# Routing decisions of an expert layer: one comparison each, the arm that is usual placed straight behind it, and two pieces of shared work placed ahead

## Chip, cores and metric

The kernel runs on one core of a Trainium2 chip. The metric is the device time of one execution in microseconds. Five engines run their own instruction streams: TensorE (PE in the profile, its weight loads PEld), VectorE (DVE), ScalarE (ACT), GpSimd (POOL) and SyncE (SP, which issues nearly all DMAs). [...]

## What is computed

A two-layer backbone over 256 latent and 256 context tokens of width 1024. Each layer mixes tokens (windowed attention, pooling, retention, one output projection) and then applies a gated channel mixer: dense in layer 0, and in layer 1, for the 256 latent tokens, two of eight experts per token. The change lies in that last mixer:

```python
def swiglu(t, wg, wu, wd):
    return (jax.nn.silu(t @ wg) * (t @ wu)) @ wd

def moe_ffn(t, router, wg, wu, wd):
    logits = (tf @ router).astype(jnp.float32)
    top_v, top_i = lax.top_k(logits, TOP_K)          # TOP_K = 2, N_EXPERTS = 8
    top_w = jax.nn.softmax(top_v, axis=-1)
    gates = ...                                      # top_w at the two chosen experts, 0 elsewhere
    for e in range(N_EXPERTS):
        y = y + gates[:, e:e + 1] * swiglu(tf, wg[e], wu[e], wd[e])
```

All is float32. FFN_DIM is 2816, so one expert has 34.6 MB of weights.

## The kernel before

Up to the experts the program is straight. The router's products, the choice of two experts per token and the numbers of tokens per expert are computed on the chip at about 834 to 838 us of the profiled execution. What follows depends on these numbers, so the kernel reads them into registers and branches.

Each expert's weights come in 11 parts of 3 MB (`FC` = 11; a part holds 256 hidden features: gate and up in `RGU`, down in `RD`, which are the tiles `rgu` and `raw`, or in further buffers `p` for the first expert). An expert with its tokens is called a place. Place 0 is expert 0, whose weights are loaded before its number of tokens is known. Places 1 to 7 are the others by falling number of tokens, in an order that depends on how many have more than 128.

- **First decision (lines 2483 to 2495).** `number[0]`, the tokens of expert 0, is loaded into a register of every engine (`tokens_of`, line 2480), and nested conditions (lines 2484, 2485, 2492) choose one of four arms: more than 128 tokens (two blocks), at most 128, at most 64, at most 32. Each arm is a whole copy of `first_place`. It begins with `first_block(m)`: the tokens are gathered as rows by a product with a one-hot matrix `OG[0]` (`og`), copied to `HP` (`hx`), turned by transposes and multiplied by the modulation `G12`, `B12`. With m = 32, four column parts of TensorE are used side by side, 256 columns of features each. Then 11 parts are multiplied. Beside them, as generators that are advanced between the products, run `modulated` (what the other experts read), `ranks` (places and registers' contents, on DVE), `beside_first` (gathering for places 1 and 2) and `residuals`.
- **Between the decisions (lines 2499 to 2507).** SP reads seven experts' numbers and six part numbers into registers, then issues the loads of parts `FC` and `FC + 1`, the first of the next place. Every engine reads four token numbers.
- **Second decision (lines 2508 to 2528).** Nested conditions choose one of seven arms: `group` (a place of two blocks and one or two small places beside it, by turns) and `places` (one after the other). `group` begins by splitting its first part into high and low halves (`split_g`: ACT writes `ghi`, DVE writes `glo`; `split_d` does the same for the down weights) and with the product `gate_up` of the first block.

The arms stand in the program in the order of the text, an `Else` behind its `If`. The arms that ran in the profiled execution are the last `Else` of the first decision (m = 32) and the `Else` at line 2525 (`group(1, [2, 3], 32, True)`, then `places` for 4 to 7). The join behind an arm that stands last is the next instruction; behind any other arm stands an unconditional branch to the join. In the trace taken branches of both kinds appear as COMPARE_BRANCH on the line of their condition. Almost all instructions are recorded by a helper at line 280 (281 in the changed kernel).

Of the kernel before, what the change touches and what calls it, by code (L numbers as in the profile page):

```python
# [30 lines left out]
D = 1024  # L31
T = 256
# [20 lines left out]
# used all along, and by the mixers only  # L53
_CA, _NA = _table(("ident", 128), ("before", 128), ("slots", 128),
                  ("eless", 64), ("eidx", 8), ("order", 32), ("first", 8))
# [4 lines left out]
def _constants():  # L60
# [44 lines left out]
    put("first", np.where(e == 0, 1024.0, 0.0)[None, :])  # L105
    return ca, cb, cc
# [12 lines left out]
# ---------------------------------------------------------------- layouts of the inputs  # L119
# vec: per layer  b_mod 48 | ln1_g 8 | ln1_b 8 | ln2_g 8 | ln2_b 8 | pool_scale 2 | sink 8 | lg_f 4 | lg_b 4  # L120
# [7 lines left out]
def prep(x, c, ctx, c_ctx, w_mod, b_mod, w_in, attn_sink, pool_w, pool_scale, ret_log_decay_fwd,  # L128
# [13 lines left out]
    # shift and scale of the first mixer by feature tile: [tile, p, k, shift|scale, 128]  # L142
# [127 lines left out]
class Engine:  # L270
    """an engine whose instructions are noted"""
# [65 lines left out]
def build(tc, a, dbg=None):  # L337
# [19 lines left out]
    # ---- what stays on chip all along  # L357
# [3 lines left out]
    XT = con.tile([128, KT, NT], F32, name="XT")   # alpha times the residual stream, feature-major  # L361
    HH = con.tile([128, KT, NT], F32R, name="HH")  # hi and lo parts of what goes into the next product
# [34 lines left out]
    # ---- the stream of weights of the dense part: the order in which they are used  # L397
# [3 lines left out]
    def weave(ws, ms, every):  # L401
        """after the i-th of the weights every[i] of the others"""
# [7 lines left out]
    WEAVE0 = [8, 5, 3, 0]                   # beside the input projection of layer 0  # L410
    WEAVEF = [0, 2, 2, 2] + [1] * 18        # beside gate and up
# [16 lines left out]
    def split_piece():  # L428
        """take the next granule apart, a part after the other"""
# [19 lines left out]
    def split_next(ahead=1):  # L449
        """take the next granule apart, if it is a weight and less than `ahead` wait for their use"""  # L450
# [4 lines left out]
    def pump(ahead=1):  # L455
        """go on with the granule to take apart when it has come and the engines for it have nothing else to do"""
# [24 lines left out]
    def next_weights(out, hold=False):  # L481
# [3 lines left out]
        pos["held"] = hold              # nothing more is taken apart while two granules are in use  # L485
# [43 lines left out]
    fixed = {}                  # of some kinds of small tiles, those that are there by turns  # L529
# [13 lines left out]
    def scales(l, which, g=None, b=None):  # L543
        """G, B with  modulated = xn * G + B  (xn before the norm's own g, b)"""
# [21 lines left out]
    def stats(k, h, st):  # L566
        """add the feature tile k of XT into the sums of the norm"""
# [60 lines left out]
    def apply_norm(k, h, nm):  # L628
        """two feature tiles from k on"""
# [9 lines left out]
    def modulate(k, h, gb, slot=None):  # L639
        """xn * G + B for two feature tiles, where their lo part comes later"""  # L640
# [12 lines left out]
    def feed(h, nm, gb):  # L653
        """a half of the tokens, normed and modulated, to where the products read it"""
# [9 lines left out]
    # ------------------------------------------------------------------ the mixer  # L664
# [13 lines left out]
    def open_late(t, eng):  # L678
        """what is not needed by the first part of the input projection"""
# [18 lines left out]
    def decay(l, DJ):  # L698
        """the decays of the retention, within a stream (DL) and from the context to the latents (DC)"""
# [30 lines left out]
    def chunked(t, w, i, s):  # L730
        """128 columns of the input projection for the tokens s, in four parts; the bank goes to t["out"]"""
# [35 lines left out]
    def values_flip(t, b, m0, n):  # L767
        """the values from feature-major to token-major"""
# [206 lines left out]
    def finish(t):  # L975
        """hi and lo parts of the mixed heads, once the input projection has read what they replace"""
# [18 lines left out]
    def sums(h, sts, done):  # L995
        """the sums of the norm of a half of the tokens, each feature tile after its residual is in"""
# [965 lines left out]
    def first_place(m, again, side, before=True):  # L1962
# [5 lines left out]
        if before:  # L1968
            first_block(m)
# [579 lines left out]
```

## Time and profile before

| what | value |
|---|---|
| time, median of 3 runs | 1625.1 us (1619.96 to 1629.07) |
| span of the profiled execution | 1624.5 us |
| PE busy | 1482.4 us (91%) |
| DVE busy | 741.4 us (46%) |
| ACT busy | 614.2 us (38%) |
| DMA | 398.67 MB, mean 245 GB/s |
| chain that ended last | PE 78%, DVE 9%, ACT 5%, DMA 4%, issue 3% |

The span lies 0.6 us below the median, so a sum made against the profiled execution is carried over by adding 0.6 us. In the page's 40 slices of 40.6 us PE is busy nine tenths or more in most; it falls off where the layers' attention is and around the two decisions. "Issue" in the chain is time in which an engine waited for nothing that the profile shows. The experts' stage runs from about 838 us to the end.

### The profile page before, as it was taken

To read this page: it belongs to the slowest core of one execution; us is meant where nothing else is said; L and a number is where in the kernel's file an instruction comes from. 1 tells how busy PE (TensorE), PEld (TensorE's weight loads), DVE (VectorE), ACT (ScalarE), POOL (GpSimd) and SP (SyncE) were. 2 spreads that over 40 slices of the span, in tenths; PEclk is the share of its full clock that TensorE was granted. 3 is DMA by queue.
4 is the path that set the end of the run, shared out by engine and by line. 5 is a ranking of instruction groups with operands and counts; after the bars stand their busy time and mean duration, and the time that the engine had idled before them with its cause. 6 is when DMAs were issued, how large, how long until landed. Compare 5 with 4: busy or idle time off the path is not lost.

```text
span 1624.5 us, 25303 instructions
## 1 busy us (share of the span) xinstructions
PE 1482.4 (91%) x10390; PEld 1088.8 (67%) x10390; DVE 741.4 (46%) x1426; ACT 614.2 (38%) x1121; POOL 93.8 (6%) x105
## 2 busy tenths in 40 slices
PE   6989999999999999887968499999998879999986
PEld 4646677777777788675746377777774458878643
DVE  4664456223223343666435344243323158888412
ACT  3464444522222343355531133232321047767301
POOL 2310002000000420100000100000000000000120
PEclk9999999999999999999988799999999999999999
DMA  9444223554444332231468689999998998988894
GB/s 380 169 157 182 103 104 108 210 202 170 175 173 164 121 128 92 100 133 43 173 270 349 255 316 374 373 361 378 358 378 318 372 370 310 362 329 326 336 398 197
DMA packets 45727, 398.67 MB, mean 245 GB/s; under 512 B 5600, under 2 KB 5856, under 8 KB 8960
## 3 DMA queue, kind: packets, MB, share of 16 engines
q1 hardware_dynamic: 44640, 391.97, 62.5%
q0 software_dynamic: 640, 4.26, 0.7%
q8 instruction: 94, 1.54, 0.4%
q14 instruction: 65, 0.53, 0.1%
q10 hardware_dynamic: 288, 0.36, 0.1%
HBM read 395.53 MB, written 1.05 MB: 244 GB/s over the span
## 4 chain that ended last, share of the span: by engine, by line
PE 78%; DVE 9%; ACT 5%; DMA 4%; issue 3%; SPq 0%; ACTq 0%; POOL 0%; DVEq 0%; POOLq 0%
PE bk L280 40%; PE b L280 38%; DMA rgu<-in_moe_dram 2%; DVE nm L280 2%; DVE XT L280 2%; ACT pexp L280 2%; DVE wl L280 1%; DMA raw<-in_wmod_dram 1%; DVE pexp L280 1%; DMA ar<-in_wm_dram 1%; ACT wh L280 1%; ACT pair L280 1%; DVE HL L280 0%; DVE hx L280 0%; DVE b L280 0%
## 5 line engine op out<-in xcount | busy, mean ns | idle before, releaser
L280 PE MATMUL b<-HH,wh 128*128 128x512 f32 (+1 forms) x752 | 268.3, 357 | 7.9 <-ACT wh L280 6.5
L280 PE MATMUL b<-HL,wh 128*128 128x512 f32 (+1 forms) x752 | 258.7, 344 | 1.1 <-DVE HL L280 1.1
L280 PE MATMUL b<-HH,wl 128*128 128x512 f32 (+1 forms) x752 | 259.0, 344 | 0.7 <-DVE wl L280 0.6
L280 DVE TENSOR_TENSOR wl<-raw,wh 128x512 fp32r<-128x512 f32 x228 | 150.5, 701 | 125.1 <-ACT wh L280 124.9
L280 PE MATMUL bk<-ghi,HL 128*128 128x512 f32 x528 | 182.3, 408 | 20.5 <-ACT ghi L280 20.5
L280 PEld LDWEIGHTS b<-HH,wh 128*128 128x128 f32 x752 | 143.5, 191 | 64.9 <-issue 26.4
L280 ACT ACTIVATE wh<-raw 128x512 fp32r<-128x512 f32 x228 | 132.9, 623 | 117.4 <-PE b L280 63.3
L280 DVE TENSOR_TENSOR glo<-rgu,ghi 128x1024 fp32r<-128x1024 f32 x132 | 154.7, 1218 | 28.6 <-ACT ghi L280 28.4
L280 PEld LDWEIGHTS b<-HH,wl 128*128 128x128 f32 x752 | 143.6, 191 | 19.4 <-DVE wl L280 2.2
L280 PEld LDWEIGHTS b<-HL,wh 128*128 128x128 f32 x752 | 143.8, 191 | 17.1 <-DVE HL L280 1.9
L280 ACT ACTIVATE hx<-bk 128x256 f32<-128x256 f32 (+2 forms) x88 | 27.7, 315 | 306.9 <-PE bk L280 301.9
L280 ACT ACTIVATE ghi<-rgu 128x1024 fp32r<-128x1024 f32 x132 | 131.2, 1051 | 30.4 <-issue 18.7
L280 DVE TENSOR_TENSOR hx<-hx,bk 128x256 f32<-128x256 f32 (+2 forms) x88 | 29.5, 335 | 236.8 <-ACT hx L280 236.8
L280 PEld LDWEIGHTS bk<-ghi,HL 128*128 128x128 f32 x528 | 101.6, 192 | 49.9 <-issue 22.9
L280 PE MATMUL bk<-dhi,SP 128*128 128x512 f32 x352 | 119.5, 400 | 0.0
L280 PE MATMUL b<-h,wh 128*128 128x512 f32 (+1 forms) x384 | 111.9, 375 | 0.0
L280 PE MATMUL bk<-glo,HL 128*128 128x512 f32 x264 | 105.8, 401 | 2.0 <-DVE glo L280 2.0
L280 DVE TENSOR_TENSOR H<-H,b 128x512 f32<-128x512 f32 x22 | 15.1, 687 | 167.5 <-PE b L280 157.4
L280 DVE TENSOR_TENSOR dlo<-raw,dhi 128x1024 fp32r<-128x1024 f32 (+1 forms) x55 | 78.7, 1433 | 15.8 <-ACT dhi L280 15.8
L280 PE MATMUL bk<-rgu,hx 128*32 128x128 f32 (+1 forms) x1376 | 80.6, 315 | 5.4 <-DVE hx L280 2.9
L280 PEld LDWEIGHTS b<-h,wh 128*128 128x128 f32 x384 | 69.8, 188 | 16.4 <-issue 2.5
L280 PEld LDWEIGHTS bk<-rgu,hx 128*32 128x32 f32 (+1 forms) x1376 | 55.0, 122 | 37.6 <-issue 14.5
(329 smaller groups left out, 2178.6 us busy)
## 6 DMA issues: line engine op xcount, KB each, us to landing
rgu<-in_moe_dram SPq DMA_DIRECT2D x81, 2048.0 KB, 9.7
raw<-in_moe_dram SPq DMA_DIRECT2D x80, 1024.0 KB, 7.6
raw<-in_wmod_dram SPq DMA_DIRECT2D x40, 1024.0 KB, 4.8
raw<-in_fgu_dram SPq DMA_DIRECT2D x22, 1024.0 KB, 5.5
p<-in_moe_dram SPq DMA_DIRECT2D x16, 1024.0 KB, 14.7
raw<-in_wout_dram SPq DMA_DIRECT2D x12, 1024.0 KB, 4.8
raw<-in_fd_dram SPq DMA_DIRECT2D x11, 1024.0 KB, 4.8
raw<-in_wib_dram SPq DMA_DIRECT2D x9, 1024.0 KB, 4.9
```

The costliest lines, as they stand in the source:

```text
L280: r = f(*args, **kw)
```

## The change

The first decision now hangs on one number, computed on DVE (`kind`: how many of 32, 64 and 128 are exceeded), the second likewise (`over`, `C1`, an arm's number from 0 to 6). Each decision compares it once with the usual arm's number; that arm stands directly behind the comparison, and the other arms behind it, in a chain of further comparisons. `first_block` no longer depends on the arm: it gathers 128 tokens whatever their number, and stands ahead of the first condition. The first product of place 1 (`next_first`: the splits of part `FC`, `gate_up` of its first block, `split_d`) stands ahead of the second condition; `group` and `places` skip it. Between the decisions SP reads one expert's number, issues the loads of part `FC`, reads two part numbers, issues those of part `FC + 1`, and reads the other ten registers after that. Comments were taken out as well.

```diff
-    V.tensor_copy(C0, b[:, 2 * E:2 * E + 1])
+    kind = rt.tile([128, 4], F32, name="kind")
+    V.tensor_scalar(kind[:, :3], cst("steps"), b[:, 2 * E:2 * E + 1], None, op0=OP.is_lt)
+    V.reduce_sum(kind[:, 3:], kind[:, :3], axis=AX.X)
+    V.tensor_copy(C0, kind[:, 3:])
...
-    def first_block(m):
...
+    def first_block():
+        og = OG[0].bitcast(F32)
+        for h in range(2):
             for i in range(2):
-                for j in range(n):
...
+                P.matmul(halved(BK[h]), lhsT=og[:, i], rhs=XN[:, i, 2 * h:2 * h + 2], start=i == 0, stop=i == 1)
+        for h in range(2):
+            if h:
+                S.activation(HP[h], BK[h], AF.Copy)
             else:
+                V.tensor_copy(HP[h], BK[h])
+            for c in range(4):
+                P.transpose(BK[2 + h][:, 128 * c:128 * c + 128], HP[h][:, 128 * c:128 * c + 128], IDENT)
+        x, b = (t.rearrange("p (k q) -> p k q", q=128) for t in (HP[0], BK[2]))
+        for t, r, op in ((b, G12, OP.mult), (x, B12, OP.add)):
+            V.tensor_tensor(x, t, r[:, 0:4, 0:1].to_broadcast([128, 4, 128]), op)
+        for k in range(4):
+            c = slice(128 * k, 128 * k + 128)
+            S.activation(HP[1][:, c], BK[3][:, c], AF.Identity, scale=G12[:, 4 + k, 0:1], bias=B12[:, 4 + k, 0:1])
...
-        if s == 1:
+        if s > 1:
+            run(split_g(u0, 0, 2))
...
+        else:
             one_hot_few(pos_of(few[0]), m)
             from_stash(m)
...
-        V.tensor_copy(CNTI[:, :2], BP[:, 4:6])
+        V.tensor_scalar(over[:, 0:2], BP[:, 4, 3:5], 64.0, None, op0=OP.is_gt)
+        V.tensor_scalar(over[:, 2:3], BP[:, 4, 3:4], 32.0, None, op0=OP.is_gt)
+        V.scalar_tensor_tensor(over[:, 3:4], many[:, 5:6], 1.0, many[:, 3:4], op0=OP.add, op1=OP.mult)
+        V.scalar_tensor_tensor(over[:, 2:3], over[:, 1:2], 2.0, over[:, 2:3], op0=OP.mult, op1=OP.max)
+        V.scalar_tensor_tensor(over[:, 3:4], over[:, 3:4], 3.0, over[:, 2:3], op0=OP.add, op1=OP.subtract)
+        V.scalar_tensor_tensor(over[:, 3:4], over[:, 3:4], over[:, 0:1], over[:, 2:3], op0=OP.mult, op1=OP.add)
+        V.scalar_tensor_tensor(C1, over[:, 3:4], 1.0, many[:, 1:2], op0=OP.add, op1=OP.mult)
+        V.tensor_copy(CNTI[:, 1:2], BP[:, 5:6])
...
+    def arms(arm, usual, bodies, shared):
+        shared()
+        with tc.If(arm == usual, preferred_fallthrough_block=True) as c:
+            bodies[usual]()
+        with c.Else():
+            one_of(arm, [x for x in bodies.items() if x[0] != usual])
...
+    arms(arm_of(C0[0:1, 0:1], 4), 0, {0: lambda: first(32), 1: lambda: first(64), 2: lambda: first(128), 3: first_twice},
+         first_block)
...
-    for s in range(1, E):
-        eid[s] = nc.values_load(CNTI[0:1, 1, s:s + 1], engines=[ET.SP], min_val=0, max_val=E - 1)
...
-    number.update({s: tokens_of(s) for s in (1, 3, 4, 5)})
...
+    expert_of(1)
+    load_gu(FC)
+    load_d(FC)
+    parts_of(1)
+    load_gu(FC + 1)
+    load_d(FC + 1)
+    arm = arm_of(C1[0:1, 0:1], 7)
+    def next_first():
+        for s in range(2, E):
+            expert_of(s)
+        for s in (3, 5):
+            parts_of(s)
         for i in range(2):
+            run(split_g(FC, i, 2))
+            gate_up(FC, 1, range(4 * i, 4 * i + 4), BK[6])
+        run(split_d(FC))
...
+    arms(arm, 1, {0: lambda: places([(s, False) for s in range(1, E)], [], True),
+                  1: lambda: places(few_ends, group(1, [2, 3], 32, True)),
...
+                  5: two_groups, 6: three_groups}, next_first)
```

On PE the first decision stands like this before. `SELR` is the router's choice, `XT,og` the gathering product, `CA,hx` a transpose of the gathered rows, `rgu,hx` the first gate and up product. The rows with the last width of 32 are the arm that ran; it stands last of the four.

```order
L280 MATMUL b<-SELR,SP 128x8 x2
L2480 TENSOR_LOAD C_6481
L2484 COMPARE_AND_BRANCH
L2485 COMPARE_AND_BRANCH
L280 MATMUL bk_6512<-XT,og 128x512 x2
...
L2485 UNCONDITIONAL_BRANCH
L2492 COMPARE_AND_BRANCH
L280 MATMUL bk_6512<-XT,og 64x512 x4
...
L2492 UNCONDITIONAL_BRANCH
L280 MATMUL bk_6512<-XT,og 32x256 x8
L280 MATMUL bk_6514<-CA,hx 128x128 x2
L280 MATMUL bk_6516<-rgu_5029,hx 32x128 x32
```

The gathering and its transposes now come between the register load and the one comparison, and the arm of width 32 comes straight behind it. On PE, now:

```order
L281 MATMUL b<-SELR,SP 128x8 x2
L2483 TENSOR_LOAD C_6481
L281 MATMUL bk_6515<-XT,og 128x512 x2
L281 MATMUL bk_6516<-XT,og 128x512 x2
L281 MATMUL bk_6517<-CA,hx 128x128 x4
L281 MATMUL bk_6518<-CA,hx 128x128 x4
L2498 COMPARE_AND_BRANCH
L281 MATMUL bk_6519<-rgu_5029,hx 32x128 x32
```

Eight products of 32 by 256, which ran four side by side, became four of 128 by 512, and two transposes became eight.

On PE the end of the first place and the second decision stand like this before. `os,HL` brings the first place's outputs to the tokens, `ghi,HL` is the first product of the next place.

```order
L280 MATMUL bk_6519<-os_6501,HL 128x256 x4
L2492 UNCONDITIONAL_BRANCH
L2480 TENSOR_LOAD CNTI x4
L2508 COMPARE_AND_BRANCH
L2509 COMPARE_AND_BRANCH
L2510 COMPARE_AND_BRANCH
L280 MATMUL bk_6518<-ghi_8991,HL 128x512
...
L2523 UNCONDITIONAL_BRANCH
L280 MATMUL bk_6518<-ghi_8991,HL 128x512
```

The register loads follow the first place's arm directly, and three comparisons at lines 2509, 2520 and 2523 lead to an arm far down. On PE, now:

```order
L281 MATMUL bk_6522<-os_6504,HL 128x256 x4
L2498 UNCONDITIONAL_BRANCH
L2490 COMPARE_AND_BRANCH
L281 MATMUL bk_6519<-rgu_5029,hx 64x256 x16
...
L2490 UNCONDITIONAL_BRANCH
L2483 TENSOR_LOAD C_6540
L281 MATMUL bk_6521<-ghi_8972,HL 128x512
...
L2498 COMPARE_AND_BRANCH
L281 MATMUL bk_6519<-IDR,og 128x128 x2
```

Behind the usual arm of the first decision there is now an unconditional branch over the three other arms, 990 matmuls on PE, 440 instructions on DVE and 142 on ACT; the 24 matmuls of the first product stand ahead of the second comparison, whose usual arm follows it.

## Rows read from the trace of the kernel before

**Rows 1.** Chain of work that ended last, both decisions: start us, us, what.
```profile
840.85 8.91 issue
...
914.88 6.04 issue
...
927.51 4.90 issue
...
932.57 1.06 ACT ghi L280
...
933.72 1.24 DVE glo L280
...
935.00 13.31 PE bk L280 x103
```

**Rows 2.** Branches by line: duration ns min/median/max, first and last start us.
```profile
L2484 PEldq COMPARE_BRANCH  x1: 6414/6414/6414, 838.0 to 838.0; - x1
L2484 DVEq COMPARE_BRANCH  x1: 72/72/72, 838.1 to 838.1; - x1
...
L2484 ACTq COMPARE_BRANCH  x1: 55/55/55, 839.8 to 839.8; - x1
...
L2492 ACTq COMPARE_BRANCH  x1: 45/45/45, 840.3 to 840.3; - x1
L2492 DVEq COMPARE_BRANCH  x1: 56/56/56, 843.9 to 843.9; - x1
L2492 PEldq COMPARE_BRANCH  x1: 5072/5072/5072, 844.5 to 844.5; - x1
...
L2508 PEldq COMPARE_BRANCH  x1: 70/70/70, 916.2 to 916.2; - x1
...
L2509 PEldq COMPARE_BRANCH  x1: 6232/6232/6232, 916.3 to 916.3; - x1
```

**Rows 3.** Timeline from the first decision: start us, us, engine, operation, idle before.
```profile
837.39 0.47 DVE L280 TENSOR_SCALAR og<-CA,NAT 128x128 fp32r<-128x128 f32 x2
...
849.76 1.94 PE L280 MATMUL bk<-XT,og 128*32 128x256 f32 x16 [12.64 <-issue]
...
852.34 0.69 PE L280 MATMUL bk<-CA,hx 128*128 128x128 f32 x2 [0.64 <-DVE hx L280]
...
853.78 3.64 PE L280 MATMUL bk<-rgu,hx 128*32 128x128 f32 x64 [0.76 <-PE bk L280]
...
859.00 1.08 PE L280 MATMUL bk<-rgu,hx 128*32 128x128 f32 x32
...
865.44 0.69 DVE L280 TENSOR_TENSOR XT<-XT,bk 128x512 f32<-128x512 f32 x1
```

**Rows 4.** Stretches: busy us of PE, PEld, DVE, ACT, POOL; granted clock, DMA share, GB/s.
```profile
838.00:849.50 11.50, 0.00 (x0) 0.00 (x0) 0.00 (x0) 2.80 (x5) 0.00 (x0) 0.51 0.58 231
853.50:857.50 4.00, 3.72 (x65) 3.37 (x66) 0.18 (x1) 1.16 (x5) 0.00 (x0) 0.50 0.02 4
933.60:940.50 6.90, 6.27 (x14) 4.62 (x15) 6.78 (x5) 4.67 (x5) 0.00 (x0) 0.50 0.19 44
1000.00:1200.00 200.00, 199.94 (x1998) 150.70 (x2000) 78.22 (x118) 64.26 (x97) 0.00 (x0) 1.00 0.93 369
```

**Rows 5.** Timeline of DVE and PE behind the ranking of the experts.
```profile
877.70 0.17 DVE L280 SCALAR_TENSOR_TENSOR steps<-steps 128x7 f32<-128x7 f32 x1
...
878.96 0.67 PE L280 MATMUL bk<-IDR,og 128*128 128x128 f32 x2 [3.50 <-DVE og L280]
```

**Rows 6.** Register loads of lines 2480 and 2500, columns as in rows 2.
```profile
L2480 ACTq TENSOR_LOAD <-CNTI x4: 275/284/289, 913.4 to 914.4; - x4
...
L2480 PEldq TENSOR_LOAD <-CNTI x4: 300/315/327, 914.5 to 915.8; - x4
L2480 DVEq TENSOR_LOAD <-CNTI x4: 299/310/321, 915.4 to 916.5; - x4
...
L2500 SPq TENSOR_LOAD <-CNTI x7: 262/264/284, 896.8 to 900.6; - x7
```

More of the change, by code (lines that the diff above doesn't have):

```diff
@@ L54 @@
 _CA, _NA = _table(("ident", 128), ("before", 128), ("slots", 128),
-                  ("eless", 64), ("eidx", 8), ("order", 32), ("first", 8))
+                  ("eless", 64), ("eidx", 8), ("order", 32), ("first", 8), ("steps", 3))
 _CC, _NC = _table(("j", 384), ("sel", 128))
@@ L105, in _constants @@
     put("first", np.where(e == 0, 1024.0, 0.0)[None, :])
+    put("steps", np.array([[32.0, 64.0, 128.0]]))
     return ca, cb, cc
@@ L1959, in scatter, with first_place @@
                 yield
-    def first_place(m, again, side, before=True):
+    def first_place(m, again, side):
         f = Few(m, lambda k: HX[k // 2][:, 128 * (k % 2):128 * (k % 2) + 128], sil.rearrange("p k n -> p (k n)"), KEPT[0],
@@ L2117, in from_stash, with places @@
             V.tensor_tensor(XL[i][..., :m], xs[:, k4, 0, :m].bitcast(F32), xs[:, k4, 1, :m].bitcast(F32), OP.add)
-    def places(todo, side):
+    def places(todo, side, begun=False):
         kinds = dict(todo)
@@ L2172, in places @@
                     from_stash(64, XE[s % 2])
+                if begun:
+                    begun, behind = False, u
+                    continue
                 if not few:
@@ L2313, in hand_over @@
             one_hot_of(nxt, then)
-        run(split_g(u0, 0, 2))
-        gate_up(u0, 1, range(0, 4), BK[6])
-        run(split_g(u0, 1, 2))
-        load_gu(u0 + 2)
-        gate_up(u0, 1, range(4, 8), BK[6])
-        run(split_d(u0))
-        if s == 1:
+        if s > 1:
+            run(split_g(u0, 0, 2))
+            gate_up(u0, 1, range(0, 4), BK[6])
+            run(split_g(u0, 1, 2))
+            load_gu(u0 + 2)
+            gate_up(u0, 1, range(4, 8), BK[6])
+            run(split_d(u0))
+        else:
             one_hot_few(pos_of(few[0]), m)
@@ L2431, in build @@
     few = rt.tile([128, 1], F32, name="few")
+    over = rt.tile([128, 4], F32, name="over")
+    C1 = rt.tile([128, 1], I32, name="C1")
     steps = rt.tile([128, 3, E], F32, name="steps")
@@ L2491, in build, with arm_of, one_of @@
-    with c0.Else():
-        with tc.If(number[0] > 32) as c6:
-            first_place(64, False, chain(modulated(), ranks(), beside_first(64), residuals()))
-        with c6.Else():
-            first_place(32, False, chain(modulated(), ranks(), beside_first(32), residuals()))
+    def arm_of(src, n):
+        return nc.values_load(src, engines=mybir.ALL_ENGINES, min_val=0, max_val=n - 1)
+    def one_of(arm, bodies):
+        if len(bodies) == 1:
+            bodies[0][1]()
+            return
+        with tc.If(arm == bodies[0][0]) as c:
+            bodies[0][1]()
+        with c.Else():
+            one_of(arm, bodies[1:])
@@ new lines, in arms, with expert_of, parts_of @@
+    def arms(arm, usual, bodies, shared):
+        shared()
+        with tc.If(arm == usual, preferred_fallthrough_block=True) as c:
+            bodies[usual]()
+        with c.Else():
+            one_of(arm, [x for x in bodies.items() if x[0] != usual])
+    def expert_of(s):
+        eid[s] = nc.values_load(CNTI[0:1, 1, s:s + 1], engines=[ET.SP], min_val=0, max_val=E - 1)
+    def parts_of(s):
+        for i in range(2):
+            lookup[FC * s + 1 + i] = nc.values_load(CNTI[0:1, 2 + i, s:s + 1], engines=[ET.SP], min_val=0, max_val=NU - 1)
@@ L2496, in build, with first, first_twice @@
+    def first(m):
+        first_place(m, False, chain(modulated(), ranks(), beside_first(m), residuals()))
+    def first_twice():
+        first_place(128, True, chain(modulated(), ranks(), residuals(), gather_out(0, OG[0], gates_of(0), halves(BK[0], BK[1])(0))))
+        whole(1)
+        first_place(128, False, beside_first(128))
+    arms(arm_of(C0[0:1, 0:1], 4), 0, {0: lambda: first(32), 1: lambda: first(64), 2: lambda: first(128), 3: first_twice},
+         first_block)
     GHI, GLO = ([wr.tile([128, 2048], F32R, name=f"{n}{i}", tag=f"g{3 * j + i}") for i in range(3)]
@@ L2527, in build @@
-    with c1.Else():
-        places([(s, False) for s in range(1, E)], [])
+    expert_of(1)
[10 more added lines that the diff above has]
+            parts_of(s)
+        for i in range(2):
+            run(split_g(FC, i, 2))
+            gate_up(FC, 1, range(4 * i, 4 * i + 4), BK[6])
+        run(split_d(FC))
```

74 lines of the change are left out of this document (11 added, 63 removed).

## The prediction

> **What bounds the kernel now.** I read the chain of waits first, because the change only touches the two places where the program branches. In the chain a piece called "issue" is time in which nothing that the profile records held the engine. Over most of the experts' stage there is none: between 1000 and 1200 us PE is busy 199.94 of 200 us [rows 4], so the stage is bound by PE, with transfers close behind (DMA share 0.93). At the decisions the chain shows holes: 8.91 us from 840.85, and three pieces from 914.88, the last of 4.90 us from 927.51 [rows 1]. Behind the first hole PE starts the gathering at 849.76 and the first gate and up product at 853.78 [rows 3]; behind the second DVE starts `glo` at 933.72, and PE works on from 935.00 [rows 1].
>
> Next I looked up the branches by line, to see what fills the holes [rows 2]. A comparison that is passed costs 0.07 us on PE (line 2508). A branch that is taken far ahead costs PE 6.41 us (line 2484), 5.07 us (2492) and 6.23 us (2509). On DVE the record is short, but line 2492 follows line 2484 only 5.8 us later (838.1 to 843.9). On ACT the same two lines lie 0.5 us apart: the arm jumped over has only 110 ACT instructions. So a far jump costs 5 to 6.4 us on every engine that makes it, and a near one half a microsecond. Two are taken at the first decision and three at the second, one after the other.
>
> [...]
>
> **Part 1, the first decision.** Removed: two far jumps on PE ahead of the gathering. Added: `kind`, its sum and a conversion on DVE ahead of `og`, one of which replaces a copy; dependent small operations take about 0.2 us, so 0.4 us. `og` then ends at 837.39 + 0.47 + 0.4 = 838.3 [rows 3], and PE may gather at once, having passed no branch.
>
> The gathering itself becomes dearer. Before, 16 records of 256 columns ran four side by side, in 1.94 us. Now 8 records of 512 columns run one behind the other, which is 16 steps of 256 columns in place of 4. At the lower clock a step is 1.94 / 4 = 0.49 us by that row, or 0.46 by the gate product (64 records of 128 columns, four side by side, in 3.64 us): 16 steps are 7.8 or 7.3 us, and half of that if the clock were up. I take 7.3, since rows 4 show the clock down at 838, and come to 845.6. Copying the first half to SBUF lies under the second half's product. Then four transposes (two took 0.69, so about 1.2), and two DVE operations on 512 columns at 0.69 each [rows 3]: the gate product starts at about 848.3 in place of 853.78. That is 5.5 us.
>
> The clock gives a little more. PE now has work from 838.3 on, so I expect it up again by 848, and the first 64 gate records then take 2 x 1.08 = 2.2 us, not 3.64: 1.5 us. The transfers that follow are issued as each buffer is done with, so they move with PE.
>
> Then a loss. `ranks` gets seven more DVE operations for `over` and `C1`. PE waits 3.50 us for DVE right behind them [rows 5], so nothing hides them; at about 0.17 to 0.2 us each that is 1.3 us. First decision: 5.5 + 1.5 - 1.3 = 5.7 us. Bounds: 9 us if the gathering runs at the upper clock, 4 us if the clock stays down through the gate product.
>
> **Part 2, from the first place to the next.** Here "the usual arm straight behind" has a price. Before, the usual arm stood last and ran into the join. Now a branch over three arms stands behind it, and it is far on PE (990 matmuls) and DVE (440 instructions). So one far jump stays. I lay the engines out on the old time axis, with register loads as marks of when each sequencer arrives [rows 6]:
>
> - PE arrives at 914.5, jumps for about 6.3 us, loads one register (0.3): ready at 921.1.
> - DVE arrives at 915.4, jumps for 5.8, loads one register (0.3): ready at 921.5.
> - ACT arrives at 913.4. Its jump covers 142 instructions, against 110 that were near. If near, `ghi` is written by 915.3; if far, 913.4 + 6.2 + 0.3 + 1.06 = 921.0, the last of these from [rows 1]. Either way it is not the last.
> - SP reads one register ahead of the first loads of part `FC`, not thirteen (seven of them from 896.8 to 900.6), so the weights come no later than before. Queued behind its new ten register loads are the loads of part `FC + 2`, which wait for `glo` anyway.
>
> DVE is last: `glo` starts at 921.5, not 933.72. That is 12.2 us, with 11.6 if DVE pays PE's 6.4. Behind it the first product runs ahead of the second comparison, which each engine passes for 0.07 us. The product starts at the lower clock as before, so nothing changes there. All loads that the next turn needs have landed before the old start, so everything from here to the end moves as it is.
>
> [...] A far jump shows as 5 to 6.4 us and a near one as 0.5 [rows 2]. [...]
>
> **Sum.** 5.7 + 12.2 = 17.9 us. 1624.5 - 17.9 = 1606.6 for the profiled execution, and 0.6 more for the median: **1607 us**, 1.1% faster.
>
> **Rivals.**
> - A, the exit jump is near or hidden. Then DVE starts `glo` behind its own last sums, at about 917 (its fourth register load was at 916.5 [rows 6]): 16.7 us in place of 12.2, and 1602.7 us. For it: ACT's near jump. Against: the distance on DVE and PE is larger than that of every jump that cost 5 us or more at the first decision (300 on DVE, 320 matmuls on PE).
> - B, passing a comparison into a long arm costs as much as a jump, since reading ahead stops at a condition. The 0.07 us of line 2508 was measured between two neighbouring instructions, so it does not exclude this. Price: about 5 us at the first decision and 6.2 us at the second: 17.9 - 11.2 = 6.7 us gain, 1618.4 us.
> - C, the second gain is given back, because the holes let transfers fill the buffers and the stage then lives on that lead. 1624.5 - 5.7 + 0.6 = 1619.4 us. For it: DMA share 0.93. Against: PE hardly ever waits there, and at 933.6 to 940.5 the DMA share is 0.19, so the lead had been complete well before it was used.
> - D, slower. The reading ahead does not recover after the comparison that is passed, and each engine pays a fetch at every block of code in the usual arm of the second decision (3387 matmuls on PE), at 5 us apiece. It decides from six such fetches on: five end at 1632, within 0.5% of before, six at 1607 + 30 = 1637 us. Against: the same arm, entered by a jump, runs with no such holes [rows 4].
>
> **How the numbers follow.** Forecast 0.67, A 0.12, B 0.10, C 0.08, D 0.03. The forecast's own bounds are 17.9 with 3.4 more or 2.3 less, so about 1604 to 1610, and the three runs of before spread over 9 us, which widens it to 1600 to 1614. A lies inside. To leave out no more than two in ten I go to 1617, the lower edge of B and C. A measurement of this kernel can tell about 0.5% from no change, that is 1617 us: faster 0.82 (forecast, A, a part of B), same 0.15, slower 0.03.
>
> **What would show it.** In the profile of after: PE's gathering at 838 to 839, taking about 7 us at a granted clock near 0.5, and the first gate product at about 848; no far branch on PE ahead of it. At the end of the first place, some 6 us earlier than now, a branch on line 2498 of 5 to 6.4 us on PE, and as long a gap on DVE, with a short one on ACT if near; then `glo` some 18 us earlier than 933.72, and comparisons passed in well under 0.1 us. From there every stretch should look the same, shifted. I am wrong if the exit branch is short (A), if a gap follows the comparisons (B), if PE waits for transfers in the stage where it did not (C, D), or if the gathering takes far more or less than 7 us.

## The result and the profile after

The changed kernel takes 1601.18 us in the median of 4 runs (1599.23 to 1603.32), the kernel before 1624.09 beside it (4 runs): a ratio of 0.9865, 95% interval 0.9839 to 0.9892, that is 22.9 us less. The forecast was 1607, with 1600 to 1617 as its range: right in sign, and 5.8 us too high.

The profiled execution took 1599.23 us with a span of 1597.4. PE is busy 1478.6 us (before 1482.4), 93% of the span instead of 91%. All numbers of lines grow by one in the helper (281 for 280).

First the branches, by line as in [rows 2] (duration in ns as minimum/median/maximum, first and last start), and the register loads behind them, as in [rows 6]. Line 2498 holds both decisions' comparisons and the branches out of the usual arms, so each engine has four records there.

```profile
L2498 PEldq COMPARE_BRANCH  x4: 75/1712/7054, 843.4 to 1583.0; - x4
L2498 DVEq COMPARE_BRANCH  x4: 51/54/56, 843.9 to 1591.1; - x4
L2498 ACTq COMPARE_BRANCH  x4: 34/38/39, 844.2 to 1590.5; - x4
...
L2483 DVEq TENSOR_LOAD <-C x2: 326/435/544, 836.7 to 910.1; - x2
L2483 PEldq TENSOR_LOAD <-C x2: 312/402/493, 836.7 to 910.8; - x2
...
L2483 ACTq TENSOR_LOAD <-C x2: 295/391/487, 838.1 to 908.4; - x2
```

A passed comparison costs PE 75 ns (the minimum; the first one, at 843.4, took 98). The 7054 ns are the branch out of the first place. The fourth record on PE, at 1583.0, is the branch out of the second decision's usual arm (3.33 us); the kernel before has one there too (line 2523 at 1610.0, 4.35 us). On DVE and ACT the record of a branch is short whatever it costs; there the price shows in when the next instruction comes, the register load at 910.1 and 908.4.

The timeline at the first decision, to be held against [rows 3] (start, us, engine, operation, what ended the idle time before):

```profile
835.36 0.61 PE L281 MATMUL b<-SELR,SP 128*128 128x8 f32 x4 [2.68 <-DVE SELR L281]
...
837.45 5.22 PE L281 MATMUL bk<-XT,og 128*128 128x512 f32 x8 [1.48 <-DVE og L281]
...
844.66 1.95 PE L281 MATMUL bk<-rgu,hx 128*32 128x128 f32 x64 [0.65 <-PE bk L281]
...
847.56 1.08 PE L281 MATMUL bk<-rgu,hx 128*32 128x128 f32 x32
...
868.42 0.69 PE L281 MATMUL bk<-IDR,og 128*128 128x128 f32 x2 [4.41 <-DVE og L281]
```

The hole of 12.64 us ahead of the gathering is gone, the gathering takes 5.22 us, and the first gate product 1.95 instead of 3.64. The router's product stands at 836.52 in the profile before: this execution came 1.16 us sooner to the place where the change begins, and this has to be taken off each difference of two start times at the first decision.

The timeline at the second decision, from the last output of the first place (`HL`) on:

```profile
902.58 0.47 ACT L281 ACTIVATE HL<-bk,GS 128x256 fp32r<-128x256 f32 x1 [3.42 <-PE bk L281]
...
904.34 2.48 DVE L281 TENSOR_TENSOR XT<-XT,bk 128x512 f32<-128x512 f32 x4 [0.78 <-PE bk L281]
908.83 3.90 ACT L281 ACTIVATE ghi<-rgu 128x1024 fp32r<-128x1024 f32 x4 [5.78 <-issue]
910.61 4.63 DVE L281 TENSOR_TENSOR glo<-rgu,ghi 128x1024 fp32r<-128x1024 f32 x4 [3.78 <-ACT ghi L281]
...
911.33 0.77 PE L281 MATMUL bk<-ghi,HL 128*128 128x512 f32 x1 [6.93 <-ACT ghi L281]
```

The waits are put down to `ghi`, but ACT itself stands for 5.78 us without anything to wait for that the profile shows ("issue"): it was in its branch, and so were PE and DVE. The chain of waits, to be held against [rows 1], names a transfer at this place:

```profile
901.09 7.96 DMA rgu<-in_moe_dram
909.16 0.63 issue
...
911.33 13.04 PE bk L281 x104
```

This is to be doubted: ACT wrote the first `ghi` from the same part at 908.83, before that transfer's end, and two kernels below start it right behind the first place. The transfer only ended while the engines were branching.

Windows (busy us of PE, PEld, DVE, ACT, POOL; granted clock, DMA share, GB/s), to be held against [rows 4]:

```profile
837.40:842.70 5.30, 5.25 (x10) 2.42 (x11) 0.69 (x1) 2.24 (x5) 0.00 (x0) 0.70 1.00 416
844.60:846.60 2.00, 1.94 (x65) 1.77 (x66) 0.00 (x0) 1.02 (x3) 0.00 (x0) 1.00 0.00 0
...
904.50:911.90 7.40, 0.57 (x2) 0.30 (x2) 3.62 (x6) 3.07 (x4) 0.00 (x0) 0.56 0.89 356
911.90:916.00 4.10, 4.10 (x11) 3.28 (x11) 4.10 (x4) 2.63 (x2) 0.00 (x0) 0.54 0.07 28
976.00:1176.00 200.00, 199.93 (x1975) 150.25 (x1977) 78.20 (x118) 64.30 (x97) 0.00 (x0) 1.00 0.93 367
```

The clock came up within the gathering (0.70 on average over it) and was 1.00 for the gate product. The group's long stretch is as full as before (199.93 of 200 us).

### The profile page after: what moved, and what is told of

Same layout as the page of the kernel before. It is cut to its first block, busy times and chain, and to the rows that moved or that the text cites. A ratio compares the mean times of both kernels' runs of the same rounds, so it can differ in the third digit from the quotient of the medians.

```text
span 1597.4 us, 25278 instructions
## 1 busy us (share of the span) xinstructions
PE 1478.6 (93%) x10388; PEld 1085.5 (68%) x10388; DVE 743.9 (47%) x1435; ACT 614.9 (38%) x1122; POOL 93.8 (6%) x105
## 5 line engine op out<-in xcount | busy, mean ns | idle before, releaser
L281 DVE TENSOR_TENSOR glo<-rgu,ghi 128x1024 fp32r<-128x1024 f32 x132 | 154.8, 1219 | 16.0 <-ACT ghi L281 15.9
L281 PEld LDWEIGHTS b<-HL,wh 128*128 128x128 f32 x752 | 143.3, 191 | 17.2 <-DVE HL L281 1.9
L281 ACT ACTIVATE hx<-bk 128x256 f32<-128x256 f32 (+3 forms) x89 | 28.3, 318 | 304.6 <-PE bk L281 304.6
L281 PE MATMUL bk<-rgu,hx 128*32 128x128 f32 (+1 forms) x1376 | 77.1, 305 | 4.6 <-DVE hx L281 2.9
L281 PEld LDWEIGHTS b<-h,wh 128*128 128x128 f32 x384 | 69.9, 188 | 16.3 <-issue 2.5
L281 PEld LDWEIGHTS bk<-dhi,SP 128*128 128x128 f32 x352 | 66.1, 188 | 17.3 <-issue 1.6
```

Of the source, the lines that this page charges most:

```text
L281: r = f(*args, **kw)
```

## The experiments

To compare kernels whose profiles begin with different offsets I measure each from marks within it: **A** from the start of the router's last products (`SELR`, four in one row) to the first gate product; **B** from the same start to the last `HL` on ACT, the end of the first place; **C** from there to the first product `rgu,hx` of the group. B + C is the whole stretch in which the change lies. What lies ahead of A and behind C is the same work in all kernels, but for 14 idle products ahead of A in the two kernels named after them and the branch out of the second decision's usual arm, which the kernel without decisions lacks. The kernel before took 1623.9, 1623.8 and 1621.7 us on the three chips that ran the experiments, so medians of different rows compare to about 2 us.

| kernel | A | B | C | B + C | median, us (runs) |
|---|---|---|---|---|---|
| before | 17.3 | 76.9 | 32.9 | 109.8 | 1624.1 (4) |
| after | 9.3 | 67.2 | 19.8 | 87.0 | 1601.2 (4) |
| first decision alone | 9.5 | 65.8 | 37.8 | 103.6 | 1619.5 (10) |
| second decision alone | 17.4 | 76.3 | 15.7 | 92.0 | 1608.7 (4) |
| layout alone | 6.2 | 66.8 | 19.9 | 86.7 | 1601.5 (4) |
| moves alone | 17.2 | 75.3 | 36.6 | 111.9 | 1626.6 (10) |
| no decisions | 9.1 | 67.0 | 16.3 | 83.3 | 1599.2 (4) |
| first usual arm last | 12.1 | 71.3 | 15.9 | 87.2 | 1600.1 (4) |
| the same with a hint | 11.8 | 71.1 | 16.0 | 87.1 | 1602.9 (4) |
| the same, gathering in the arm | 12.8 | 71.8 | 15.7 | 87.5 | 1602.8 (1) |
| one other arm | 9.2 | 67.0 | 19.3 | 86.3 | 1596.5 (1) |
| idle products at the router | 5.3 | 66.2 | 20.7 | 86.9 | 1598.0 (4) |
| idle products at two places | 5.3 | 63.9 | 19.8 | 83.6 | 1597.4 (5) |
| after, again | 9.4 | 67.5 | 19.8 | 87.3 | 1601.0 (4) |

My theory was that each far branch costs every engine that takes it 5 to 7 us, that this is the time of fetching instructions, and that what was moved ahead of the decisions is worth little by itself. The rivals: the moved work is what gains, because it covers the branches; or the branch that is left (out of the first place) is free.

**One decision at a time.** The kernel before with the first decision's new form, and the changed kernel with the first decision's old form:

```diff
-    number = {0: tokens_of(0)}
-    with tc.If(number[0] > 64) as c0:
...
+    arms(arm_of(C0[0:1, 0:1], 4), 0, {0: lambda: first(32), ...}, first_block)
+    number = {}
```

> The kernel before with the first decision alone changed: one number, one comparison, the usual arm behind it, the block gathered ahead; the second decision stays nested. My theory: a branch that is taken far costs each engine that takes it 5 to 7 us, and nothing else of the change is worth much. Then the first decision gains as in the changed kernel (about 9.7 us), and gives 6 to 7 us back where the usual arm now has to jump over three others; the three jumps of the second decision stay. About 1620 us, that is 3 to 4 us under the kernel before. Rival 1, the branch out of the arm costs nothing or hides behind the loads of the next place: 1614 us. Rival 2, the gains at the two places depend on each other: no gain at all, 1624 us.

> The changed kernel with the first decision as it was before (nested conditions, the arm that runs last of the four, its gathering inside), the second decision as changed. My theory: no branch out of the first place, so glo of the next place starts some 6 us sooner behind the first place's end than in the changed kernel: of the second decision 18 us are gained, not 12, and of the first none. About 1606 us. Rival 1, the branch out costs nothing: 12 us gained, 1612 us. Rival 2, glo waits for its weights once the branch is gone: 1609 to 1612 us, with a wait for a transfer in the place of the branch.

The first alone took 1619.47 us (ratio 0.9983, 0.9963 to 1.0004), the second alone 1608.68 (0.991, 0.9888 to 0.9932). The first decision gains 76.9 - 65.8 = 11.1 us in B and gives 37.8 - 32.9 = 4.9 back in C, where the branch out now stands ahead of the three old ones. With the second alone C is 15.7, and 4.1 us shorter than in the changed kernel. So the branch out is not free. It costs 4.1 us and not the 6 that I expected, because without it DVE still has its four sums to do (until HL + 4.2 us):

```profile
911.71 0.47 ACT L281 ACTIVATE HL<-bk,GS 128x256 fp32r<-128x256 f32 x1 [3.42 <-PE bk L281]
912.16 3.90 ACT L281 ACTIVATE ghi<-rgu 128x1024 fp32r<-128x1024 f32 x4
...
913.47 2.48 DVE L281 TENSOR_TENSOR XT<-XT,bk 128x512 f32<-128x512 f32 x4 [0.78 <-PE bk L281]
...
915.87 2.35 DVE L281 TENSOR_TENSOR glo<-rgu,ghi 128x1024 fp32r<-128x1024 f32 x2
```

These are rows of the timeline of the second decision alone: `ghi` follows `HL` at once, so no transfer is late there.

**The layout alone, and the moves alone.** In the first, gathering and first product are inside the arms again; in the second, the nested conditions of before stand behind the moved work.

```diff
 layout alone:
     def first(m):
+        first_block(m)
...
-        for i in range(2):
-            run(split_g(FC, i, 2))
-            gate_up(FC, 1, range(4 * i, 4 * i + 4), BK[6])
-        run(split_d(FC))
 moves alone:
+    first_block()
+    with tc.If(number[0] > 64) as c0:
...
+    next_first()
+    with tc.If(number[1] > 128) as c1:
```

> The changed kernel without the two moves: one comparison and the usual arm behind it stay, but the gathering is inside each arm again (32 tokens, four products side by side) and the first product of the next place is inside the second decision's arms. My theory: a comparison that is passed costs under 0.1 us, so there is nothing that the moved work covers, and the gathering of 32 is cheaper than that of 128 by some 4 us: 1597 us. Rival: the moved work covers the comparison (reading ahead stops at it), so without it a gap of some us follows each comparison: 1602 to 1612 us.

> The kernel with the two moves alone: the gathering and the next place's first product stand ahead of the decisions, which are nested with the usual arms last, as in the kernel before. My theory: PE goes through its work and its branches one after the other, so moving work from behind a jump to ahead of it shifts the jump and removes nothing: the first gate product at 853 to 855 us as before, and at the second decision 2 to 5 us gained, as DVE and ACT jump beside PE's product. 1619 to 1623 us. Rival: the jumps hide behind the moved work: 1602 to 1608 us.

The layout alone took 1601.47 us (0.9873, 0.9843 to 0.9903), the same as the whole change; the moves alone 1626.58 (1.0016, 1.0002 to 1.0029), no gain at all, where I had expected 2 to 5 us. So the layout is the change, and the rival of the covering work falls. Moving alone even lost in C: PE's three branches now stand behind its first product and take 5.3, 7.9 and 5.1 us, 2.4 us more than the same three before (6.2, 4.7 and 5.0). On its timeline of PE, the last piece of that product and the next one:

```profile
924.74 0.39 PE L281 MATMUL bk<-ghi,HL 128*128 128x512 f32 x1
939.92 0.66 PE L281 MATMUL bk<-IDR,og 128*128 128x128 f32 x2 [14.79 <-issue]
```

I had expected 1597 of the layout alone, and it missed that for a reason worth a look. It is 3.1 us shorter in A, but only 0.4 of it is left at the end of B. Its timeline and its windows:

```profile
838.82 1.93 PE L281 MATMUL bk<-XT,og 128*32 128x256 f32 x16 [1.62 <-DVE og L281]
...
842.83 3.64 PE L281 MATMUL bk<-rgu,hx 128*32 128x128 f32 x64 [0.75 <-PE bk L281]
846.39 1.12 PE L281 MATMUL bk<-CA,G 128*128 128x128 f32 x4
847.30 1.06 PE L281 MATMUL bk<-CA,B 128*128 128x128 f32 x4
```

```profile
838.80:842.80 4.00, 2.62 (x18) 0.96 (x19) 1.00 (x3) 2.38 (x7) 0.00 (x0) 0.50 1.01 422
842.80:848.20 5.40, 5.38 (x72) 4.78 (x72) 0.87 (x2) 1.11 (x5) 0.00 (x0) 0.50 0.46 153
```

The granted clock is 0.50 all through, and the gate product takes 3.64 us. It was busy for 2.62 of the 4.0 us up to that product; in the changed kernel the dear gathering kept it busy for 5.25 of 5.30 us, and the clock was up (1.00) for the gate product. That the moved gathering pays for itself in this way, not by covering a branch, is tested below under the clock.

**No decisions at all.** Only the two usual arms are in this program; the other nine are left out.

```diff
-        with tc.If(arm == usual, preferred_fallthrough_block=True) as c:
-            bodies[usual]()
-        with c.Else():
-            one_of(arm, [x for x in bodies.items() if x[0] != usual])
+        bodies[usual]()
```

> The changed kernel without any decision: only the two usual arms stand in the program, one after the other; the other nine arms are left out. My theory: what is left of the decisions in the changed kernel is the one branch out of the first place, and it costs what the kernel with the second decision alone saved between the first place's end and the next group's first product, 19.8 - 15.7 = 4.1 us: 1597 us. Rival 1: that branch is hidden in the sum, 1601 us. Rival 2: a long program or a passed comparison costs more than the traces show (reading instructions ahead), 1593 us or less, with the difference spread over the arms.

1599.18 us (0.9843, 0.9814 to 0.9872). B + C is 3.7 us shorter than in the changed kernel, 3.5 of them in C: what the decisions still cost is the branch out; no more than 0.2 us is left in B, where the first comparison is passed. Of the medians' difference, 2 us, the sign alone agrees; the intervals overlap.

**What a far branch waits for.** The usual arm behind the other three again, so that the far branch leads into it and none leads out; the same with a prefetch hint (the two lines of `mark_branch_hint_location`, in this kernel alone); and the same without the hint and with the gathering inside the arm (what is `shared` is then empty), so that PE branches 6 us sooner.

```diff
+        if usual == 0:
+            for e in (ET.PE, ET.DVE, ET.Activation):
+                tc.mark_branch_hint_location("d0", arm, engines=[e])
+            shared()
+            with tc.If(arm != 0, preferred_fallthrough_block=True, label="d0") as c:
+                one_of(arm, [x for x in bodies.items() if x[0] != 0])
+            with c.Else():
+                bodies[0]()
+            return
         shared()
```

> The changed kernel with the first decision's usual arm put behind the other three: one comparison, a far branch into the arm behind the gathering, and no branch out of it. My theory: the far branch moves from the arm's end to its start. PE comes to it 8.2 us after the router's last product and takes 5 to 6.5 us, so the gate product starts 14 us after that product and not 9.3 (4.7 lost), at the lower clock again (1.7 lost); at the end 4.1 us are gained: 1603 to 1604 us. Rival: the branch into the arm hides beside the gathering (PE's instructions are issued ahead of their execution), 1597 us.

> The kernel of the run before, with a prefetch hint for that branch on PE, VectorE and ScalarE, placed directly behind the load of the register that decides it, ahead of the gathering; the register's value says whether the branch will be taken. My theory: the price of a far branch is that the instructions at its target have to be fetched when it is taken, and the jump itself costs nothing. With the fetch begun 5 us earlier, beside the gathering, the branch takes under 1 us on PE, the gate product starts about 9.4 us after the router's last product, and there is no branch out: 1597 us. Rival: the jump itself costs 5 us whatever has been fetched, 1603 to 1604 us as in the run before.

> The kernel with the first decision's usual arm last and the gathering of 32 inside it, so that PE takes the far branch straight behind the register load, at a time when the loads of the first expert's weights keep the DMA engines full. My theory: the instructions at the target come by DMA and queue behind those loads, so the branch takes 6.4 us on PE, as it did at this time in the kernel before, and not the 3.5 to 3.8 us that it took 6 us later with the DMA share at a quarter; the gate product starts 12.5 to 13 us after the router's product. Rival: the price is shorter because one comparison stands there and not two, 3.7 us, and the gate product starts at 10 us.

They took 1600.11 (0.9837, 0.9809 to 0.9866), 1602.91 (0.9858, 0.9817 to 0.99) and, in one run, 1602.75 us. PE's branch by line in the three, in this order, with the hint's record behind the second, and a window over each of the three branches:

```profile
L2499 PEldq COMPARE_BRANCH  x1: 3746/3746/3746, 843.9 to 843.9; - x1
...
L2501 PEldq COMPARE_BRANCH  x1: 3482/3482/3482, 844.1 to 844.1; - x1
L2583 PEldq BRANCH_PREFETCH_HINT  x1: 44/44/44, 838.0 to 838.0; - x1
...
L2514 PEldq COMPARE_BRANCH  x1: 6649/6649/6649, 840.9 to 840.9; - x1
```

```profile
843.85:847.60 3.75, 0.66 (x4) 0.41 (x4) 1.17 (x2) 1.50 (x4) 0.00 (x0) 1.00 0.05 15
...
844.10:847.60 3.50, 0.66 (x4) 0.42 (x4) 1.19 (x2) 1.51 (x4) 0.00 (x0) 1.00 0.04 14
...
840.95:847.60 6.65, 0.00 (x0) 0.00 (x0) 0.00 (x0) 2.31 (x5) 0.00 (x0) 0.53 0.88 355
```

The branch into the usual arm takes 3.5 to 3.75 us when the DMA engines are idle (share 0.04 and 0.05) and 6.65 when they are full (0.88). This is what I forecast for the third, and what I had missed for the first: I had expected 5 to 6.5 us there, and the quarter at which I put its DMA share afterwards is 0.05 over the branch itself. These kernels differ in more than the transfers: in the third the arm also holds the gathering, and the granted clock is 0.53, not 1.00. But the trace records the fetching itself, as packets of kind "instruction". The DMA queues in the third kernel, from 840.95 to 845.10 and from 845.12 to 846.26:

```profile
q1 hardware_dynamic: 240, 1.71, 100.0%
q14 instruction: 2, 0.02, 1.1%
...
q1 hardware_dynamic: 53, 0.43, 95.1%
q8 instruction: 1, 0.02, 6.2%
```

Queue q8 has a packet of 16 KB inside each far branch of PE. Here it begins 4.2 us after the branch, takes 1.1 us, and the branch ends 1.3 us behind it; in the first kernel, with the arm last, it begins after 1.1 us, takes 1.3, and the branch ends 1.4 us behind it. So the difference is the wait of the fetch, and it goes with the load of queue q1, which moves the weights. The other profiles say the same. In 26 of the 38 far branches on PE in the fourteen profiles one such packet lies inside; it takes 0.9 to 1.4 us and the branch ends 1.3 to 1.5 us behind it, while the wait ahead of it is 1.0 to 1.6 us at a DMA share of 0.05 or less and 3.0 to 4.7 us at 0.88 or more (3.3 to 3.9 and 5.3 to 7.1 us in all). In the other twelve two packets lie inside. Most of these follow close on another far branch, and even with a share of 0.35 or less those took 4.7 to 5.6 us: line 2492 of the kernel before, with a share of 0.09, has both packets between 845.50 and 847.70.

```profile
q8 instruction: 2, 0.03, 10.9%
```

The hint ran on PE at 838.0, 6 us ahead, and the branch was 0.26 us shorter: no effect that two single profiles can tell. My forecast of that run failed. No packet of q8 begins between the hint and the branch; the one that PE waited for begins 1.0 us after the branch, as without the hint. So the hint fetched nothing for PE. Whether it named the wrong outcome, no run here tells.

For the sum it makes no difference at which end the far branch stands: B + C is 87.2 with it at the entrance and 87.0 with it at the exit.

**Distance.** Two of the three other arms are left out, so that the branch out passes fewer instructions.

```diff
-            one_of(arm, [x for x in bodies.items() if x[0] != usual])
+            one_of(arm, [x for x in bodies.items() if x[0] != usual][:1 if usual == 0 else None])
```

> The changed kernel with only one other arm (64 tokens) behind the first decision's usual one; the two arms of 128 tokens and of two blocks are left out. The branch out of the usual arm then passes 313 matmuls on PE, 135 instructions on VectorE and 41 on ScalarE. My theory: the distance decides between near (0.5 us) and far (5 us and more). ScalarE's branch, far over 142 instructions and near over 110 before, is near again; PE's is far or nearly so (320 matmuls were far before); VectorE's 135 lie between the two of ScalarE and are open. If VectorE and PE stay far, nothing is gained: 1600 us. Rival: a branch out of an arm is far whatever it passes, ScalarE's too.

```profile
L2498 PEldq COMPARE_BRANCH  x4: 75/1750/6456, 842.1 to 1580.3; - x4
...
901.23 0.47 ACT L281 ACTIVATE HL<-bk,GS 128x256 fp32r<-128x256 f32 x1 [3.40 <-PE bk L281]
902.11 3.90 ACT L281 ACTIVATE ghi<-rgu 128x1024 fp32r<-128x1024 f32 x4 [0.41 <-issue]
...
905.40 4.62 DVE L281 TENSOR_TENSOR glo<-rgu,ghi 128x1024 fp32r<-128x1024 f32 x4
...
909.38 0.77 PE L281 MATMUL bk<-ghi,HL 128*128 128x512 f32 x1 [6.33 <-DVE glo L281]
```

Branches and timeline: ACT stands 0.41 us and DVE is held by its own sums, so both branches are near (41 and 135 instructions), and the rival falls. PE's, over 313, is far with 6.46 us (902.3 to 908.8), and it alone keeps C at 19.3; the wait of PE's product is put down to `glo`, but the first of the four pieces of `glo` was done before PE's branch ended. On ACT the limit lies between 110 instructions (near, before) and 142 (far, after), on DVE between 135 (near, here) and 300 (far, before). If both have the same limit, it lies between 135 and 142; no run tests that. On PE 313 are too many. The single time, 1596.49 us, says nothing about 0.5 us.

**The clock.** Since the clock took back the cheap gathering's gain, I kept PE busy with products that nobody reads: 14 ahead of the router's last product and 8 behind it, with the gathering inside the arm; then 24 more where PE waits for the ranking.

```diff
+    idle = bank()
+    for _ in range(14):
+        P.matmul(idle[:, :128], lhsT=IDENT, rhs=IDENT, start=True, stop=True)
...
+        for _ in range(24):
+            P.matmul(BK[1][:, 384:512], lhsT=IDENT, rhs=IDENT, start=True, stop=True)
```

> The changed kernel with the gathering of 32 tokens inside the arm (as in the kernel with the layout alone), and with 22 products of 128 by 128 that nobody reads, 14 ahead of the router's last product and 8 behind it, while PE waits for DVE. My theory: the gathering of 128 was no loss, because its work brought the granted clock up in time for the first gate product; with PE kept busy beforehand the cheap gathering needs no such help. The gate product starts 5 us after the router's last product (6.2 with the layout alone, 9.3 in the changed kernel) and takes 1.95 us (3.64 and 1.95): 1597 us. Rival: the 3.64 us of the gate product with the cheap gathering are not the clock's doing but its weights' or its waits', and stay: 1601 us.

> The kernel with the gathering of 32 in the arm and 22 idle products around the router's, and 24 more idle products of 128 by 128 in the 4.4 us in which PE waits for DVE's ranking (ahead of IDR,og). My theory: what is left at the first decision beside the branch out is the clock. The gate product starts 5.3 us after the router's product at the upper clock (4 us against the changed kernel), and the four products behind IDR,og take 1.07 to 1.08 and 0.85 us instead of 1.93 and 1.30 (2.4 us): from the router's product to the end of the first place 61 us, not 67.2, and 1595 us in all. Rival: the clock falls somewhere else instead, as it did 22 us further on in the run with the 22 products alone: 66 us, and 1598 us.

> The changed kernel itself beside the others on the same chip: 1601 us, and the spread of its runs. [...]

Timeline of the first and a window of its later part:

```profile
838.40 1.07 PE L281 MATMUL bk<-XT,og 128*32 128x256 f32 x16
...
841.31 1.95 PE L281 MATMUL bk<-rgu,hx 128*32 128x128 f32 x64 [0.76 <-PE bk L281]
```

```profile
889.60:896.60 7.00, 6.91 (x90) 5.18 (x94) 2.71 (x8) 0.22 (x1) 1.08 (x2) 0.51 0.45 152
```

The gathering takes 1.07 us, the gate product 1.95, and A is 5.3 us, as forecast: the clock was the reason. Then the clock fell to 0.51 at 889.6 to 896.6, where the changed kernel has 1.00, and 3.0 of the 4 us were lost again. With the second filling the four products behind `IDR,og` run at the upper clock (1.00), and the lower one comes at 892 to 896 (0.57):

```profile
871.00:877.00 6.00, 5.54 (x120) 4.01 (x112) 2.95 (x15) 1.35 (x7) 0.00 (x0) 1.00 1.02 418
892.00:896.00 4.00, 4.00 (x62) 3.12 (x66) 1.16 (x4) 0.00 (x0) 0.00 (x0) 0.57 0.26 57
```

So theory and rival both hold in part: B is 63.9 us, between the 61 and the 66 expected; 0.9 of it are my own 24 products, which were still running when `IDR,og` could have started (30.0 us behind the router's product, 29.1 without them). The times were 1598.01 (0.9821, 0.979 to 0.9851) and 1597.44 us (0.9849, 0.9829 to 0.9869), beside 1600.95 (0.9871, 0.9852 to 0.989) for the changed kernel on the second one's chip. The kernel with both fillings is 3.5 us under the changed one on the same chip, with overlapping intervals. In the repeated profile of the changed kernel B is 67.5 and C 19.8, as in the first: within this stretch two executions agree to 0.3 us, and the clock falls at the same places (0.50 at 868 to 872 in both); in the first it is at 0.50 for 3.4 us from 837.2, for 6.8 from 867.9 and for 10.3 from 905.4. The spread of the times is made elsewhere: in the fourteen profiles the router's product stands between 834 and 839.5 us, and the stretch behind C takes 674 to 680. So these two profiles do not show the clock at the decisions making the spread; what makes it was not looked for.

## Why the prediction was right, and where its sizes were off

**First decision, 5.7 us forecast, 9.7 measured** (76.9 - 67.2). The term that was mis-sized is the gathering.
- Its start was right: 2.1 us behind the router's product, 1.8 forecast.
- The 7.3 us for it were wrong; it took 5.22. I took the lower clock for all of it, from [rows 4], where PE had idled for 11 us. Here PE idled 1.5 us, and the clock rose in the middle of the gathering's own work (0.50 from 837.2 to 840.6, 1.00 behind it). What follows up to the gate product took 2.0 us, not 2.7. So the gate product came 8.0 us sooner, not 5.5. The kernel with the first decision alone agrees (9.5 from the router's product, 9.3 here).
- The clock behind it was forecast to give 1.5 us and gave 2.3, as the modulation's transposes ran at the upper clock too (third gate product 10.3 us sooner, 847.56 for 859.00 with the 1.16 taken off).
- The seven new DVE operations were forecast to cost 1.3 us; `IDR,og` lost 0.9 (868.42 for 878.96).

I had given 9 us as the upper bound of this term, for a gathering at the upper clock. The true value lies above it: a bound has to be taken for all that hangs on the same assumption together, and the clock's later gift hung on it as well.

**Second decision, 12.2 us forecast, 12.3 measured** at `glo` (20.3 - 8.0 us behind `HL`). The branch out is far on PE and DVE, as forecast, and DVE comes at 910.1, 5.6 us behind its branch (5.8 forecast). PE's 7.05 us lie above the 5 to 6.4 that I took for every far jump: its packet waited 4.7 us, where those of the kernel before waited 3.8 us at most. That PE then came last, not DVE, cost little: its first product starts 0.7 us behind `glo`, and by its second product the gain is 12.3 us again. ACT's, over 142 instructions, was far too (5.8 us), which I had left open and which changed nothing, since it arrives first. Then 0.8 us more came while the clock was down: it stayed so until 915.7, 3.8 us behind the start of the second product, and before until 940.5, 5.5 us behind it.

**The price of a taken branch.** In the traces a far branch on PE ends 1.3 to 1.5 us behind a packet of kind "instruction" on queue q8 where one such packet lies inside (26 of 38); the exit, whose packet waited 4.7 us, took 7.05. The prediction took one price for all far jumps, 5 to 6.4 us; the prices run from 3.3 to 7.9 us, by how long the fetch waits and whether a second packet stands beside it.

**The rivals.** A (exit free, 1602.7) gives nearly the measured time, by luck and for the wrong reason: the exit costs 4.1 us (second decision alone) or 3.5 (no decisions). B fell (comparisons passed in 75 and 98 ns, with no gap behind them), C and D fell (199.93 of 200 us busy).

**The sum.** 9.7 + 13.1 = 22.8 us in the traces, for 22.9 between the medians. The spans differ by 27.1: 1.2 of the rest lie ahead of the change and 3.1 behind it, within the 5.9 by which that stretch differs from profile to profile. The 0.6 us by which I carried the sum over was wrong as well: the time is 1.8 us above the span (1599.23 and 1597.4), so by this difference the profile of before was of a run 1 to 2 us above its medians (1625.1 and 1624.1).

## What to carry over

Count the taken far branches on each engine, and price each at where it stands: on PE 3.3 to 4.4 us for one by itself when hardly any transfers ran, 4.7 to 5.6 close behind another one, 5.3 to 7.1 under a full DMA load, and under 0.1 us (70 to 98 ns) for a comparison that is passed. With one comparison per decision, one far branch was left on PE in every kernel here whose usual arm stands among others, at its entrance or its exit: with ACT and DVE near (41 and 135 instructions) and PE far (313 matmuls), C was 0.5 us shorter, and no run has all three near. Moving work from behind a branch to ahead of it shifted the branch and did not remove it. In the changed kernel it brought PE's clock up (0.70 over the gathering, 1.00 at the gate product), and in the moves alone it put the first branch where hardly any transfers ran (3.6 us for 6.4), which the dearer gathering used up: A is 17.2 us for 17.3.

## What the runs showed that I had not expected

- The dearer gathering was hardly a loss: 5.22 us of work at a rising clock, followed by a gate product of 1.95 us, is only 0.5 us behind 1.93 us of gathering followed by 3.64 us at a granted clock of 0.50 when the third gate product starts (12.2 and 11.7 us after the router's product).
- The lower clock that was avoided at the first decision came in another place in both kernels with idle products (0.51 at 889.6 to 896.6, 0.57 at 892 to 896, where the changed kernel has 1.00), with PE hardly idle in the first of them (6.91 of 7.00 us busy). Why it fell there, and not in the changed kernel, no run shows.
- The prefetch hint was carried out in 44 ns, fetched nothing for PE and left the branch at 3.48 us.
